# Order of the accumulating transfers in the GpSimd queue of an up-projection: sums of one pair interleaved with those of the next

## The chip, the cores and the metric

The kernel runs on one core of one Trainium2 chip. The metric is the time of one execution in microseconds of the device. The profile is that of one further execution, whose own time stands beside its span below.

## The reference

One layer of a diffusion backbone: a modulated input, three parallel token mixers, an output projection with residual and layer norm, and then the gated convolutional feed-forward network in which the change lies. There are 640 tokens (128 context, 512 latent), a model width of 1024 and a feed-forward width of 2816.

```python
def _conv_ffn(h, w_up, w_dw, b_dw, w_down, latent):
    a, g = jnp.split(h @ w_up, 2, axis=-1)
    ...
    conv = conv + b_dw
    return (jax.nn.gelu(conv) * g) @ w_down
...
    f = _conv_ffn(h2, p['w_up'], p['w_dw'], p['b_dw'], p['w_down'], latent)
    x = _layer_norm(alpha * x + g2 * f.astype(x.dtype), p['ln2_g'], p['ln2_b'])
```

`conv` is a 3x3 depthwise convolution on the latent grid and one of width 3 on the context.

## The kernel before

The last stage of the kernel, some 530 us of the profile, is the feed-forward network. Its width of 2816 is cut into 22 blocks j of 128 channels. For each block the up-projection makes two tiles, a (to be convolved) and g (the gate). Blocks 0 to 2 are made in the stage before, block 3 in plain form by `up_one`, and blocks 4 to 21 by `up_pair`, a *pair* each in what follows, being a and g of one block. A pair uses seven block products instead of eight (a Strassen form): tokens are cut into near (0 to 319) and far (320 to 639), the 1024 rows of the weights into a first and a second half, and sums of weight halves and of activation halves enter the products. Each product is 12 fp32r matmuls of TensorE (four tiles of 128 rows, three terms each: high times high, high times low, low times high), so a pair is 84 matmuls.

The weight sums are made by transfers that add to what they find (`onto`, line 1543, issued on GpSimd's queue, 128x512 elements each). Of a pair, `ra` and `rb` are buffers of the pool tag `sraw` (four buffers, so two pairs at a time), and `raw` is one of the streaming buffers; the first half of each is columns 0 to 511 (`f_`), the second columns 512 to 1023 (`s_`). SP loads `ra` (the weights of a, line 1559), `rb` (those of g, line 1560) and `raw` (those of g again, line 1569). The four sums are named here by number, and this text keeps to these names:

- sum1: first half of `rb` += first half of the weights of a, from memory (line 1561)
- sum2: second half of `rb` += first half of `rb` (line 1562); it needs sum1
- sum3: first half of `raw` += second half of the weights of g, from memory (line 1570)
- sum0: second half of `ra` += second half of `rb` (line 1595); it needs sum2, and it overwrites what the cast of a has read

Before TensorE can use a weight buffer, ScalarE casts it to a high part (`cast`, line 1587) and VectorE subtracts that for the low part (`low`, line 195). Per pair there are four such entries: a (`ra`), c (`rb`, after sum2), r (`raw`, after sum3) and t (the second half of `ra`, after sum0, 128x512). `advance` takes the next entry: it casts it, and leaves its low part and an *after* step to the next `settle`. The entries run one pair ahead: while `up_pair(j)` issues its seven products, a, c, r and t of pair j+1 are cast, in that order, at fixed places between the products.

The order on every engine is the order of the code here, as the stage is scheduled by hand. `up_pair` (from line 1705) goes: product with a onto xx, copy of xx by ScalarE (line 1717), second product with a, cast of the next a, then the products with c, r and t, each with copies or subtractions, and between them `pump`, which issues VectorE's taps of the convolution and, later, gelu (line 1665), gating (line 1669) and the split of the gated tile. The first product with c writes over xx and so has to wait for the copy at line 1717. At the end comes the copy at line 1743 and the cast of the next t.

Where transfers are issued in the kernel before: sum1 and sum2 of a pair right behind its loads (`load_pair`, called as *after* of t two pairs earlier), sum3 right behind its load (`load_raw`, called as *after* of r, or of a weight of the down-projection), and sum0 as *after* of a. An `rb` load needs the buffer that the low part of t has freed.

After pairs 7, 9 and 14 comes a down-projection over the blocks made so far (`down_part`): ten tiles of matmuls, whose scaled results (`ftmp`, two buffers) are added to `x1d` in memory by transfers on the same GpSimd queue. In it the entries of the next pair (a, c, then r, t) are cast at the last tile of each half.

Of the kernel before, what the change touches and what calls it, by code (L numbers as in the profile page):

```python
# [153 lines left out]
def layer_kernel(ctx, tc, wst, wada, par, cst, ftab, ttab, cond, x, state, sgub, wst_t, rows, bg, y, snew):  # L154
# [1386 lines left out]
    with tc.tile_pool(name="pu", bufs=1, reuse_waits="tile") as pu:  # L1541
# [11 lines left out]
        got_w, raws, pairs = {}, {}, {}  # L1553
        rest_raw, rest_pair, entries = [], [], []

        def load_pair(j):
            ia, ib = (plan.setdefault(("cm", "w_up", i * DFF + j * P), len(plan)) for i in range(2))
            ra, rb = pairs[j] = [pu.tile([P, 1024], F32, tag="sraw", bufs=SRAW, name=nm("sraw")) for _ in range(2)]
            nc.sync.dma_start(out=ra, in_=wst[ia])
            nc.sync.dma_start(out=rb, in_=wst[ib])  # L1560
            onto(rb[:, f_], wst[ia][:, f_])
            onto(rb[:, s_], rb[:, f_])

        def load_raw(key):
            kind, *a_ = key
            if kind == "r":
                ib = plan.setdefault(("cm", "w_up", DFF + a_[0] * P), len(plan))
                r = raws[key] = strm.tile([P, 1024], F32, tag="raw", name=nm("raw"))
                nc.sync.dma_start(out=r, in_=wst[ib])
                onto(r[:, f_], wst[ib][:, s_])  # L1570
            else:
                raws[key] = raw_weights("tm", "w_down", a_[0] * 512, 512, a_[1])
# [17 lines left out]
        def entry(key):  # L1590
            kind, *a_ = key
            if kind == "a":
                ra, rb = pairs[a_[0]]
                got_w[key], f = cast(ra)
                after = lambda: onto(ra[:, s_], rb[:, s_])
            elif kind == "c":
                got_w[key], f = cast(pairs[a_[0]][1])
                after = lambda: None
            elif kind == "t":
                got_w[key], f = cast(pairs.pop(a_[0])[0][:, s_], 512)  # L1600
                after = next_pair
            else:
                w, f = cast(raws.pop(key))
                got_w[key] = halves(w) if kind == "d" else w
                after = next_raw
            lows.append((f, after))
# [195 lines left out]
        with tc.manual_schedule(engines=MANUAL3 | {mybir.EngineType.Pool, mybir.EngineType.SP}):  # L1802
            next_pair()
            next_raw()
            next_pair()
            for j in (1, 0, 2):
                feed(j, [landed.pop((j, i)) for i in range(2)])
            advance()
            advance()
            settle()  # L1810
            next_raw()
            for kind, n in jobs:
                {"one": up_one, "pair": up_pair, "down": down_part}[kind](n)
# [114 lines left out]
```

## Time and profile before

| | us |
|---|---|
| median of 3 runs | 1302.96 |
| lowest and highest | 1300.44, 1307.67 |
| the profiled execution | 1306.42 |
| its span | 1304.6 |

| engine | busy us | share of the span |
|---|---|---|
| TensorE, matmuls | 1184.2 | 91% |
| VectorE | 887.8 | 68% |
| ScalarE | 509.9 | 39% |
| GpSimd | 91.7 | 7% |

Busy time of TensorE counts pipelined matmuls, so it is no measure of TensorE at its peak. Up to some 700 us TensorE is busy 96% to 100% of each 100 us; from 800 to 1200 us it is 74% to 83%, at a mean granted clock of 0.86 to 0.90 of full speed. That stretch holds pairs 4 to 19 and the three down-projections. In the rows below, PE is TensorE, DVE VectorE, ACT ScalarE, POOL GpSimd, and a trailing q stands for an engine's queue of instructions. A wait is attributed to the last event that the profile shows before it ends.

### The profile page before, as it was taken

To read this page: it belongs to the slowest core of one execution; us is meant where nothing else is said; L and a number is where in the kernel's file an instruction comes from. 1 tells how busy PE (TensorE), PEld (TensorE's weight loads), DVE (VectorE), ACT (ScalarE), POOL (GpSimd) and SP (SyncE) were. 2 spreads that over 40 slices of the span, in tenths; PEclk is the share of its full clock that TensorE was granted. 3 is DMA by queue.
4 is the path that set the end of the run, shared out by engine and by line. 5 is a ranking of instruction groups with operands and counts; after the bars stand their busy time and mean duration, and the time that the engine had idled before them with its cause. 6 is when DMAs were issued, how large, how long until landed. Compare 5 with 4: busy or idle time off the path is not lost. (4 is left out here: it accounts for less than half of the span.)

```text
span 1304.6 us, 19072 instructions
## 1 busy us (share of the span) xinstructions
PE 1184.2 (91%) x7535; PEld 1116.2 (86%) x7535; DVE 887.8 (68%) x1656; ACT 509.9 (39%) x844; POOL 91.7 (7%) x111
## 2 busy tenths in 40 slices
PE   9999999999999999999999996698696779867887
PEld 7999999999999999899988886687686768867876
DVE  7697576466775684988467866577664664456886
ACT  5576464334443222233235634343332431333520
POOL 0000000000000000000000002122122112211000
PEclk9999999999999999999999997799898889888989
DMA  9422212211252353534342226577675556765332
GB/s 350 167 69 68 80 49 73 73 57 50 83 197 86 109 167 129 175 112 166 97 161 98 98 99 128 137 176 132 159 135 125 135 148 119 163 146 117 123 121 84
DMA packets 54971, 161.80 MB, mean 124 GB/s; under 512 B 6233, under 2 KB 8665, under 8 KB 54881
## 3 DMA queue, kind: packets, MB, share of 16 engines
q1 hardware_dynamic: 39472, 131.22, 29.9%
q0 software_dynamic: 15408, 29.37, 13.5%
q8 instruction: 59, 0.97, 0.3%
q14 instruction: 32, 0.25, 0.1%
HBM read 136.97 MB, written 14.16 MB: 116 GB/s over the span
## 5 line engine op out<-in xcount | busy, mean ns | idle before, releaser
L195 DVE TENSOR_TENSOR wl<-raw,wh 128x1024 fp32r<-128x1024 f32 x123 | 148.0, 1204 | 84.9 <-ACT wh L219 75.9
L277 PE MATMUL up<-s,wh 128*128 128x320 f32 x216 | 76.8, 356 | 88.8 <-ACT fm L1717 88.8
L219 ACT CAST wh<-raw 128x1024 fp32r<-128x1024 f32 x83 | 85.0, 1027 | 168.3 <-PE gm L278 91.6
L277 PE MATMUL up<-go,wh 128*128 128x320 f32 (+2 forms) x384 | 124.2, 323 | 7.3 <-ACT fm L1755 6.3
L277 PEld LDWEIGHTS up<-s,wh 128*128 128x128 f32 x216 | 46.8, 217 | 93.3 <-ACT fm L1717 93.3
L278 PE MATMUL up<-go,wh 128*128 128x320 f32 (+2 forms) x384 | 123.1, 321 | 1.0 <-DVE go L195 1.0
L279 PE MATMUL up<-go,wl 128*128 128x320 f32 (+2 forms) x384 | 122.3, 318 | 0.4 <-DVE s11hv L307 0.4
L277 PE MATMUL gm<-h,wh 128*128 128x320 f32 x384 | 121.4, 316 | 0.0
L278 PE MATMUL gm<-h,wh 128*128 128x320 f32 x384 | 118.9, 310 | 0.0
L279 PE MATMUL gm<-h,wl 128*128 128x320 f32 x384 | 118.6, 309 | 0.0
L195 DVE TENSOR_TENSOR wl<-sraw,wh 128x1024 fp32r<-128x1024 f32 (+1 forms) x54 | 56.3, 1043 | 73.5 <-ACT wh L1587 73.1
L1657 DVE SCALAR_TENSOR_TENSOR cv<-fm,par,cv 128x441 f32<-128x441 f32 (+2 forms) x152 | 105.1, 691 | 1.7
L1587 ACT CAST wh<-sraw 128x1024 fp32r<-128x1024 f32 (+1 forms) x54 | 48.7, 903 | 127.4 <-DMA sraw<-sraw 101.5
L421 DVE SCALAR_TENSOR_TENSOR adac<-rawa,csil,adac 128x512 f32<-128x512 f32 x120 | 84.8, 744 | 10.3 <-DMA rawa<-in_wada 8.5
L277 PEld LDWEIGHTS up<-go,wh 128*128 128x128 f32 x384 | 76.8, 200 | 8.8 <-ACT fm L1755 6.6
L278 PEld LDWEIGHTS up<-go,wh 128*128 128x128 f32 x384 | 76.2, 199 | 2.4 <-DVE go L195 2.0
L279 PEld LDWEIGHTS up<-go,wl 128*128 128x128 f32 x384 | 75.8, 197 | 0.8 <-DVE s11hv L307 0.8
L277 PE MATMUL dn<-wh,h 128*128 128x512 f32 (+1 forms) x188 | 71.9, 383 | 2.5 <-ACT h L1671 1.6
L278 PE MATMUL up<-s,wh 128*128 128x320 f32 x216 | 74.2, 343 | 0.0
L279 PE MATMUL up<-s,wl 128*128 128x320 f32 x216 | 73.9, 342 | 0.0
L277 PEld LDWEIGHTS gm<-h,wh 128*128 128x128 f32 x384 | 72.1, 188 | 1.7 <-issue 1.2
L279 PE MATMUL dn<-wh,h 128*128 128x512 f32 (+1 forms) x188 | 71.6, 381 | 1.7 <-DVE h L195 1.6
(455 smaller groups left out, 3311.1 us busy)
## 6 DMA issues: line engine op xcount, KB each, us to landing
raw<-in_wst SPq DMA_DIRECT2D x134, 512.0 KB, 3.6
sraw<-in_wst SPq DMA_DIRECT2D x36, 512.0 KB, 4.5
rawa<-in_wada SPq DMA_DIRECT2D x32, 512.0 KB, 3.5
sraw<-sraw POOLq DMA_DIRECT2D x36, 256.0 KB, 4.2
wa<-in_wada SPq DMA_DIRECT2D x16, 512.0 KB, 8.0
x1d<-ftmp POOLq DMA_DIRECT2D x30, 256.0 KB, 4.1
sraw<-in_wst POOLq DMA_DIRECT2D x18, 256.0 KB, 4.1
raw<-in_wst POOLq DMA_DIRECT2D x18, 256.0 KB, 4.6
```

The lines of the kernel that those rows point to most:

```text
L195: V.tensor_tensor(out, src, hi.bitcast(F32), op=ALU.subtract)
L219: A.copy(wh[:, 0:n], r)
L277: PE.matmul(out, lhsT=l[0], rhs=r[0], start=start, stop=False, skip_group_check=onto)
L278: PE.matmul(out, lhsT=l[0], rhs=r[1], start=False, stop=False, skip_group_check=onto)
L279: PE.matmul(out, lhsT=l[1], rhs=r[0], start=False, stop=stop, skip_group_check=onto)
L421: MAC.scalar_tensor_tensor(acc_[:, cd], r[:, i], s_, acc_[:, cd], op0=ALU.mult, op1=ALU.add)
L1587: A.copy(wh[:, 0:n], r)
L1657: V.scalar_tensor_tensor(cg[:, r0:r1, c0:c1], ag[:, r0 + r - 1:r1 + r - 1, c0 + c - 1:c1 + c - 1], tap(r, c), cg[:, r0:r1, c0:c1], op0=ALU ...
```

## The change

The sums of the weights are no longer issued where their buffers are loaded. `load_pair` and `load_raw` put them into three lists, `sums1`, `sums2` and `sums3`, and the *after* steps take one from a list: that of a issues sum0 and then a sum1, that of r (and of a down weight) a sum2, that of t a sum3. `go` issues the next of a list, but no sum2 while the sum1 of its pair is not issued; `due` issues what an entry needs and is still in a list. At the start the first pairs' sums are issued by hand in the order shown.

```diff
--- before.py
+++ after.py
@@ -1552,14 +1552,25 @@
         jobs += [("pair", j) for j in range(10, 15)] + [("down", 2)] + [("pair", j) for j in range(15, NF)]
         got_w, raws, pairs = {}, {}, {}
         rest_raw, rest_pair, entries = [], [], []
+        sums1, sums2, sums3 = [], [], []
+
+        def go(*lists):
+            for l_ in lists:
+                if l_ and not (l_ is sums2 and sums1 and sums1[0][0] <= l_[0][0]):
+                    l_.pop(0)[1]()
+
+        def due(j, *lists):
+            for l_ in lists:
+                while l_ and l_[0][0] <= j:
+                    l_.pop(0)[1]()
 
         def load_pair(j):
             ia, ib = (plan.setdefault(("cm", "w_up", i * DFF + j * P), len(plan)) for i in range(2))
             ra, rb = pairs[j] = [pu.tile([P, 1024], F32, tag="sraw", bufs=SRAW, name=nm("sraw")) for _ in range(2)]
             nc.sync.dma_start(out=ra, in_=wst[ia])
             nc.sync.dma_start(out=rb, in_=wst[ib])
-            onto(rb[:, f_], wst[ia][:, f_])
-            onto(rb[:, s_], rb[:, f_])
+            sums1.append((j, lambda: onto(rb[:, f_], wst[ia][:, f_])))
+            sums2.append((j, lambda: onto(rb[:, s_], rb[:, f_])))
 
         def load_raw(key):
             kind, *a_ = key
@@ -1567,7 +1578,7 @@
                 ib = plan.setdefault(("cm", "w_up", DFF + a_[0] * P), len(plan))
                 r = raws[key] = strm.tile([P, 1024], F32, tag="raw", name=nm("raw"))
                 nc.sync.dma_start(out=r, in_=wst[ib])
-                onto(r[:, f_], wst[ib][:, s_])
+                sums3.append((a_[0], lambda: onto(r[:, f_], wst[ib][:, s_])))
             else:
                 raws[key] = raw_weights("tm", "w_down", a_[0] * 512, 512, a_[1])
 
@@ -1590,19 +1601,35 @@
         def entry(key):
             kind, *a_ = key
             if kind == "a":
+                due(a_[0], sums1, sums2)
                 ra, rb = pairs[a_[0]]
                 got_w[key], f = cast(ra)
-                after = lambda: onto(ra[:, s_], rb[:, s_])
+
+                def after():
+                    onto(ra[:, s_], rb[:, s_])
+                    go(sums1)
             elif kind == "c":
                 got_w[key], f = cast(pairs[a_[0]][1])
                 after = lambda: None
             elif kind == "t":
                 got_w[key], f = cast(pairs.pop(a_[0])[0][:, s_], 512)
-                after = next_pair
+
+
+                def after():
+                    next_pair()
+                    go(sums3)
             else:
+                if kind == "r":
+                    due(a_[0], sums3)
                 w, f = cast(raws.pop(key))
                 got_w[key] = halves(w) if kind == "d" else w
-                after = next_raw
+
+
+                def after():
+                    next_raw()
+                    go(sums2)
+                    if kind == "d":
+                        go(sums3)
             lows.append((f, after))
 
         def settle():
@@ -1802,13 +1829,16 @@
         with tc.manual_schedule(engines=MANUAL3 | {mybir.EngineType.Pool, mybir.EngineType.SP}):
             next_pair()
             next_raw()
+            go(sums1)
             next_pair()
+            go(sums2, sums3, sums1)
             for j in (1, 0, 2):
                 feed(j, [landed.pop((j, i)) for i in range(2)])
             advance()
             advance()
             settle()
             next_raw()
+            go(sums3)
             for kind, n in jobs:
                 {"one": up_one, "pair": up_pair, "down": down_part}[kind](n)
                 if kind == "one":
```

**GpSimd's queue in the last run of pairs.** Before the change, from sum0 of pair 18 on; `sraw_10784`, `sraw_10925`, `sraw_11066` and `sraw_11207` are rb of pairs 18 to 21, the `sraw` numbered one lower the ra of the same pair, and `raw` that of pairs 20 and 21:

```order
L1543 DMA sraw_10783<-sraw_10784 128x512
L1543 DMA raw_11038<-in_wst 128x512
L1543 DMA sraw_11066<-in_wst 128x512
L1543 DMA sraw_11066<-sraw_11066 128x512
L1543 DMA sraw_10924<-sraw_10925 128x512
L1543 DMA raw_11179<-in_wst 128x512
L1543 DMA sraw_11207<-in_wst 128x512
L1543 DMA sraw_11207<-sraw_11207 128x512
L1543 DMA sraw_11065<-sraw_11066 128x512
L1543 DMA sraw_11206<-sraw_11207 128x512
```

After the change, from the same sum on; the tiles of a pair carry numbers lower by one:

```order
L1543 DMA sraw_10782<-sraw_10783 128x512
L1543 DMA sraw_10924<-in_wst 128x512
L1543 DMA sraw_10924<-sraw_10924 128x512
L1543 DMA raw_11037<-in_wst 128x512
L1543 DMA sraw_10923<-sraw_10924 128x512
L1543 DMA sraw_11065<-in_wst 128x512
L1543 DMA sraw_11065<-sraw_11065 128x512
L1543 DMA raw_11178<-in_wst 128x512
L1543 DMA sraw_11064<-sraw_11065 128x512
L1543 DMA sraw_11206<-in_wst 128x512
L1543 DMA sraw_11206<-sraw_11206 128x512
L1543 DMA sraw_11205<-sraw_11206 128x512
```

Before, sum0 of pair 19 (`sraw_10924<-sraw_10925`) stands behind sum1 and sum2 of pair 20; now it stands ahead of both, behind sum3 of pair 20.

**GpSimd's queue at the start of the stage.** Before; `sraw_8266` and `sraw_8275` are rb of pairs 4 and 5, `raw_8271`, `raw_8289` and `raw_8355` belong to pairs 4, 5 and 6:

```order
L1543 DMA sraw_8266<-in_wst 128x512
L1543 DMA sraw_8266<-sraw_8266 128x512
L1543 DMA raw_8271<-in_wst 128x512
L1543 DMA sraw_8275<-in_wst 128x512
L1543 DMA sraw_8275<-sraw_8275 128x512
L1543 DMA sraw_8265<-sraw_8266 128x512
L1543 DMA raw_8289<-in_wst 128x512
L1543 DMA raw_8355<-in_wst 128x512
```

After, where rb of pair 5 is `sraw_8273`:

```order
L1543 DMA sraw_8266<-in_wst 128x512
L1543 DMA sraw_8266<-sraw_8266 128x512
L1543 DMA raw_8269<-in_wst 128x512
L1543 DMA sraw_8273<-in_wst 128x512
L1543 DMA sraw_8265<-sraw_8266 128x512
L1543 DMA raw_8288<-in_wst 128x512
L1543 DMA sraw_8273<-sraw_8273 128x512
L1543 DMA raw_8354<-in_wst 128x512
```

Sum0 of pair 4 (`sraw_8265<-sraw_8266`) stood behind sum2 of pair 5 and now stands ahead of it.

**GpSimd's queue in the first down-projection.** Before, from sum0 of pair 8 on; rb of pairs 8, 9 and 10 are `sraw_8709`, `sraw_8849` and `sraw_9205`, and `x1d` rows are the down-projection's own:

```order
L1543 DMA sraw_8708<-sraw_8709 128x512
L1543 DMA x1d_7123<-ftmp_9092 128x512
L1543 DMA x1d_7119<-ftmp_9111 128x512
L1543 DMA x1d_7120<-ftmp_9131 128x512
L1543 DMA x1d_7121<-ftmp_9149 128x512
L1543 DMA x1d_7122<-ftmp_9168 128x512
L1543 DMA x1d_7123<-ftmp_9198 128x512
L1543 DMA sraw_9205<-in_wst 128x512
L1543 DMA sraw_9205<-sraw_9205 128x512
L1543 DMA sraw_8848<-sraw_8849 128x512
```

After, from the same sum on:

```order
L1543 DMA sraw_8708<-sraw_8709 128x512
L1543 DMA sraw_8849<-in_wst 128x512
L1543 DMA x1d_7123<-ftmp_9091 128x512
L1543 DMA x1d_7119<-ftmp_9110 128x512
L1543 DMA x1d_7120<-ftmp_9130 128x512
L1543 DMA x1d_7121<-ftmp_9148 128x512
L1543 DMA x1d_7122<-ftmp_9167 128x512
L1543 DMA sraw_8849<-sraw_8849 128x512
L1543 DMA x1d_7123<-ftmp_9198 128x512
L1543 DMA sraw_8848<-sraw_8849 128x512
L1543 DMA sraw_9205<-in_wst 128x512
L1543 DMA sraw_9205<-sraw_9205 128x512
```

Sum1 and sum2 of pair 9 were issued during pair 7 and now stand between the down-projection's transfers; sum0 of pair 9 has moved ahead of sum1 and sum2 of pair 10.

TensorE, VectorE, ScalarE and SP have the same instructions in the same order before and after; only the numbers of the transfers that they wait for differ.

## Rows read from the trace of the kernel before

**Rows 1.** Table of waits, 780 us to the end: us in total, times, longest us.
```profile
POOL sraw L1543 <- DMA sraw<-in_wst: 146.8, 27, 11.7
ACT wh L1587 <- DMA sraw<-sraw: 101.5, 15, 12.8
...
PE up L277 <- ACT fm L1717: 88.8, 17, 10.8
...
POOL raw L1543 <- DMA raw<-in_wst: 48.7, 10, 7.5
POOL x1d L1543 <- DVE ftmp L1778: 48.1, 18, 6.3
```
**Rows 2.** Chain of waits, pair 18 to 19: start us, us, what.
```profile
1172.28 3.38 DMA sraw<-in_wst
...
1176.24 0.87 POOL sraw L1543
1177.11 4.24 issue
...
1181.90 7.02 DMA sraw<-sraw
...
1188.95 0.62 ACT wh L1587
```
**Rows 3.** Busy us (instructions) of PE, PEld, DVE, ACT, POOL; granted clock; DMA share; GB/s.
```profile
801.76:857.82 56.06, 43.17 (x252) 42.38 (x252) 39.17 (x60) 22.70 (x37) 8.71 (x10) 0.85 0.56 133
903.75:925.38 21.63, 14.12 (x84) 13.86 (x84) 15.55 (x24) 7.67 (x13) 3.48 (x4) 0.83 0.63 149
971.57:1055.06 83.49, 55.13 (x336) 54.08 (x336) 43.95 (x65) 28.89 (x47) 14.02 (x16) 0.85 0.60 142
1111.33:1209.46 98.13, 71.94 (x432) 70.62 (x430) 55.25 (x82) 36.76 (x57) 18.32 (x21) 0.86 0.62 144
1209.46:1223.67 14.21, 12.59 (x84) 12.33 (x84) 12.50 (x19) 7.78 (x13) 0.85 (x1) 1.00 0.22 54
1130.62:1191.73 61.11, 42.76 (x252) 41.97 (x252) 37.13 (x56) 23.31 (x38) 10.46 (x12) 0.84 0.58 134
867.00:900.00 33.00, 31.39 (x147) 26.02 (x145) 21.61 (x33) 7.23 (x9) 10.38 (x12) 1.00 0.76 135
925.38:937.98 12.60, 12.13 (x63) 12.04 (x64) 9.27 (x16) 6.53 (x11) 1.73 (x2) 0.75 0.65 184
1055.06:1067.67 12.61, 12.14 (x63) 12.05 (x64) 10.48 (x17) 5.87 (x10) 1.73 (x2) 0.75 0.55 155
857.82:867.81 9.99, 9.53 (x63) 9.45 (x64) 9.14 (x15) 6.22 (x11) 1.00 (x2) 1.00 0.75 215
```
**Rows 4.** ScalarE in order of time, pairs 20 and 21: start us, us, instruction, idle before.
```profile
1219.04 0.43 ACT L1743 COPY fm<-up 128x320 f32<-128x320 f32 x1 [0.85 <-PE up L279]
1219.36 0.62 ACT L1587 CAST wh<-sraw 128x512 fp32r<-128x512 f32 x1
1221.41 0.74 ACT L1665 ACTIVATE cv<-cv 128x640 f32<-128x640 f32 x1 [1.42 <-DVE cv L1657]
...
1223.67 0.42 ACT L1717 COPY fm<-up 128x320 f32<-128x320 f32 x1
...
1228.28 1.05 ACT L1587 CAST wh<-raw 128x1024 fp32r<-128x1024 f32 x1
```
**Rows 5.** VectorE in order of time, the same pairs.
```profile
1219.57 1.22 DVE L195 TENSOR_TENSOR wl<-raw,wh 128x1024 fp32r<-128x1024 f32 x1
...
1224.54 0.68 DVE L195 TENSOR_TENSOR wl<-sraw,wh 128x512 fp32r<-128x512 f32 x1
...
1226.78 1.22 DVE L195 TENSOR_TENSOR wl<-raw,wh 128x1024 fp32r<-128x1024 f32 x1
```
**Rows 6.** ScalarE in order of time, start of the stage.
```profile
788.53 1.04 ACT L1587 CAST wh<-sraw 128x1024 fp32r<-128x1024 f32 x1 [12.29 <-DMA sraw<-sraw]
...
799.80 0.62 ACT L1587 CAST wh<-sraw 128x512 fp32r<-128x512 f32 x1 [5.82 <-DMA sraw<-sraw]
```
## Prediction

> **What bounds the kernel now.** I read the table of waits of the last stage first, then the chain of waits, then the busy time by stretch, and last the order of single instructions on ScalarE and VectorE in the one pair that runs undisturbed.
>
> The waits say that TensorE stands still 88.8 us in all, at 17 of the 18 pairs, before the same matmul, for the copy at line 1717; that copy stands on ScalarE behind the cast of "t", and the casts wait 101.5 us for sums inside an `sraw` buffer. GpSimd itself waits 146.8 us for transfers into `sraw` [rows 1]. So an in-order queue of transfers sets the pace, and no engine does.
>
> The chain of waits shows the loop, here from the cast of t of pair 18 to that of pair 19: after the low part of t, the load of pair 20's rb is issued at 1172.28; its landing lets sum1 of pair 20 go at 1176.24; sum2 must await sum1, 4.24 us; and sum0 of **pair 19**, which needs nothing of pair 20, stands behind sum2 in the queue, lands 7.02 us later, and only then can t of pair 19 be cast, at 1188.95 [rows 2]. A pair's own last sum thus waits for a load and a sum of the next pair.
>
> What the loop costs is read from the stretches between the copies at line 1717, one per pair: 56.06 us for three periods, 21.63 for one, 83.49 for four and 98.13 for five, which is 259.31 us for 13 periods, 19.95 each. The fourteenth, from pair 20 to 21, where no further pair is loaded, takes 14.21 [rows 3]. In it TensorE is busy 12.59 us and VectorE 12.50, at a granted clock of 1.00 (2.4 GHz); in the others the clock is 0.83 to 0.86, that is, partly at 1.2 GHz after the stalls.
>
> **The change, part by part.** No transfer is added or removed. The rows on SP, TensorE, VectorE and ScalarE stay in their order; only GpSimd's queue is permuted, and SP's next ra load, which waits for sum0, can only start earlier. The price of an issue, 0.87 us of GpSimd [rows 2], stays, four to a pair; GpSimd was busy 10.46 us in 61.11 [rows 3], which covers it wherever it stands.
>
> *Sum0 of a pair now goes as soon as its a is split, ahead of sum1 of the next pair.* To see what is late next I lay the new order over the undisturbed pair. Count from the copy that ends pair 20, at 1219.04; in pair 21 weights of the last down-projection stand in the places of the next a, c and r. The cast of t begins 0.3 us later; the low part of r ends at 1.75; the low part of t at 6.2, which frees the buffer for the next rb load; the low part of a at 9.0; the cast of c begins at 9.2; the next cast of t is due at 14.5 [rows 4, 5]. So sum0, issued at 9.0, has 5.5 us. It has more in fact: the gelu behind t's cast waited another 1.42 us for VectorE [rows 4], so t may be late by that much free of cost, which makes 6.9. What it needs: sum1 alone took 0.87 + 4.24 us until sum2 could follow, and sum0 as the second of two took 7.02 from the end of the wait [rows 2]. With a load and at most the tail of one sum beside it, I take 5.5, nearer to the lone one. That fits.
>
> *Sum1 of the next pair now follows sum0.* Its load is issued at 6.2 and took 1176.24 - 1172.28 = 4.0 us [rows 2], so sum1 can go at about 10.3; it holds up nothing, as what stands behind it is its own sum2.
>
> *Sum2 is issued after the low part of the previous r*, at 1.75 or a little later; c needs it at 9.2, so it has 7.5 us where sums took 5.1 to 7.0. In the kernel before, it was ready most of a pair earlier. That is a wait which the change makes possible, and it costs nothing as long as a sum lands within 7.5.
>
> *Sum3 (for r) is issued after the low part of t*, at 6.2; its raw load is issued at 1.75 and must have landed, which it has by 5.8 if it takes the 4.0 us of the rb load. Before, GpSimd waited 48.7 us for raw loads, at most 7.5 at a time [rows 1]; a load of 6 us would leave it standing 1.6 here, and behind it is only sum0, due at 9.0.
>
> Nothing then keeps the pair from the 14.21 us of the undisturbed one, whose limit is VectorE's order (12.50 us busy plus two waits for ScalarE). I take 14.4, since its loads and sums now run closer together. **Pairs: 259.3 - 13 x 14.4 = 72.1 us gained.** The return of the clock is in this term, as the 14.21 were measured at 1.00.
>
> *The pairs that end a run.* Pair 9, entered after a long stall, took 12.60 us to its last copy at a clock of 0.75, and pair 14 took 12.61; pair 7, entered after a short one, took 9.99 at 1.00 [rows 3]. Pairs 9 and 14 should fall to that: **2 x 2.6 = 5.2 us gained.**
>
> *The first pair.* Its t waited 5.82 us for sum0 of pair 4, which stood behind sum2 of pair 5 and so behind sum1 of pair 5. Now it needs only its own sum2, whose landing let c be cast at 788.53; t was cast at 799.80 [rows 6]. At most the 5.8 us go; if VectorE's taps, already queued, become late instead, some 2 stay. I take **4 us gained.**
>
> *The first pair after a down-projection* inherits VectorE work: 15.55 us against 12.50 [rows 3]. That was hidden in the stall and is uncovered now; 0 to 3 us each, I take 1.6 for pairs 8, 10 and 15: **4.8 us given back.**
>
> *The down-projections.* A sum1 now stands among the accumulating transfers to x1d, and a sum2 ahead of the last of them. Both find their input landed long before, so they cost 0.87 us of issue each, and those transfers waited 48.1 us for VectorE there [rows 1], which covers it; without that cover it would be 1.7 us for each of three, 5 us.
>
> **Sum: 72.1 + 5.2 + 4 - 4.8 = 76.5 us**, and the profiled execution took 1306.4, so 1229.9, or 1230. That execution lies 3.5 us above the median of the runs shown, so a median may come out at 1226; the range takes it in.
>
> **Rivals.** *The transfers themselves become the bound.* Over three pairs the DMA engines were busy 0.58 of 61.11 us, 11.8 us a pair; the most they held over a long mixed stretch is 0.76, in the first down-projection [rows 3]. If that is their limit, a pair takes 11.8 / 0.76 = 15.5 us: 259.3 - 201.5 = 57.8, with 5.2 and 4 and nothing given back (the longer pair covers VectorE's backlog) 67, so 1239. For it: sums slowed one another, as the 7.02 shows. Against: a mean share of 0.83 is what my own forecast asks for, bursts have long gaps now, and pair 7 ran at 0.75 undisturbed. The Trainium skill, "DMA: Bandwidth & Descriptors", section "Issuing engines are not separate DMA queues", says that transfers issued by any engine run on the same 16 DMA engines and interleave; by that rule an order of issue changes who waits but not how much must be moved. The trace agrees in so far as a sum beside another took 7.02 us where one alone took 4.24.
>
> *The sums still stand in t's way*, because sum0 now waits behind sum3 for its raw load or behind sum2 of its own pair. Half of the loop's excess would stay, 17 us a pair: 259.3 - 221 = 38, with 3 for the start 41, so 1265. The 7.5 us longest wait for a raw load speak for it; that sum3 comes 2.8 us ahead of sum0 speaks against.
>
> *Slower: the wait moves from t to c.* If sum2, now issued late, lands so late that c holds up ScalarE, and with it the copies behind c, each pair waits there. The price is the lateness itself: a pair of 21 us needs a landing 6.8 us past the 7.5 it has, or 14.3, and gives 13 x 21 - 259.3 = 14 us more, so 1320. It turns slower than before at a landing of some 13.2 us. No sum in the chain took over 7.1, so little speaks for it.
>
> *It does nothing measurable*, if the sum was hidden behind a second wait of equal length, such as that for VectorE ahead of t: 1306. The undisturbed pair speaks against it.
>
> **How the numbers follow.** The forecast has 0.72, the DMA bound 0.18, the sums still in the way 0.06, slower 0.02, nothing 0.02. The forecast's own ends are 14.2 us a pair, the whole 5.8 at the start and nothing given back, 86 us, so 1221 and by the median's 3.5 some 1217; and the 5 us of uncovered issues with 3 us more behind each down-projection, 1240. With most of the DMA bound the range is 1215 to 1250; it leaves out the last three cases and the tails. About 0.5%, 6.5 us, is what a measurement of this kernel can tell from no change. Faster by more than that: 0.72 + 0.18 + 0.06 = 0.96; within it 0.02; slower by more 0.02.
>
> **What would show it right or wrong.** Right: TensorE's wait for the copy at line 1717 falls from 88.8 us to below 35; casts wait below 20 us for sums in `sraw`; the stretches of pairs show 14 to 15 us each, a clock near 1.00 and a DMA share above 0.75; in the chain of waits VectorE takes the place of the transfers. The DMA bound would show as casts of t or c waiting 1 to 2 us in each pair, with sums that take over 7 us. A new wait would show as casts from `sraw` at full width, c, waiting for a sum. I am wrong if the pairs stay above 16 us, or if the down-projections lengthen by more than 5 us each.

## The result, and the profile after

| | before | after |
|---|---|---|
| median, us | 1301.7 (4 runs) | 1232.28 (4 runs) |
| lowest and highest | 1299.67, 1307.67 | 1230.45, 1236.86 |
| the profiled execution, its span | 1306.42, 1304.6 | 1236.86, 1235.1 |
| mean granted clock | 0.958 | 0.981 |

The ratio is 0.9465, with a 95% interval of 0.9423 to 0.9506. The forecast was 1230, with a range of 1215 to 1250: it was right in sign and size. A second measurement of the same kernel beside the last experiments gave 1233.08 (0.9431, 0.9402 to 0.946).

By stage, from the starts of the near copy (line 1717 before, 1744 after) on ScalarE's timeline, in us. "Periods" are the 13 that were 56.06 + 21.63 + 83.49 + 98.13 in [rows 3]; "downs" run from the near copy of pairs 7, 9 and 14 to that of the next pair, and so hold the pair as well.

| | before | forecast | after | after, again |
|---|---|---|---|---|
| to the near copy of pair 4 | 801.8 | 797.8 | 798.2 | 797.9 |
| 13 periods | 259.3 | 192.0 | 191.0 | 188.4 |
| three downs | 148.4 | 143.2 | 149.8 | 150.2 |
| pair 20 | 14.2 | 14.2 | 14.2 | 14.2 |
| the rest | 80.9 | 80.9 | 81.8 | 79.8 |
| span | 1304.6 | 1228.1 | 1235.1 | 1230.5 |

Of the 69.5 us by which the span fell, 68.3 came from the pairs and 3.6 from the start; the downs and what follows gave some back. Windows of the changed kernel over the stretches of [rows 3] (the same columns); the first four are pairs 4 to 6, 8, 10 to 13 and 15 to 19, then comes pair 20, then the three downs:

```profile
798.23:839.62 41.39, 36.74 (x243) 35.71 (x244) 39.09 (x62) 23.04 (x37) 8.71 (x10) 1.00 0.73 178
888.90:903.38 14.48, 14.01 (x79) 14.02 (x80) 14.39 (x22) 7.67 (x14) 2.59 (x3) 0.80 0.81 188
947.97:1008.24 60.27, 53.19 (x344) 51.61 (x342) 43.78 (x65) 28.79 (x47) 14.64 (x17) 0.97 0.80 188
1064.21:1139.11 74.90, 66.43 (x432) 64.60 (x430) 56.77 (x85) 36.65 (x57) 18.83 (x23) 0.98 0.84 193
1139.11:1153.32 14.21, 12.59 (x84) 12.33 (x84) 12.51 (x19) 7.78 (x14) 1.24 (x2) 1.00 0.33 73
839.62:888.90 49.28, 41.64 (x215) 36.01 (x213) 34.49 (x54) 15.37 (x23) 13.02 (x15) 0.96 0.70 150
903.38:947.97 44.59, 41.50 (x205) 35.70 (x205) 34.02 (x51) 15.64 (x22) 12.24 (x15) 0.96 0.74 158
1008.24:1064.21 55.97, 53.87 (x254) 45.63 (x255) 32.59 (x46) 16.48 (x22) 11.19 (x14) 0.97 0.58 133
```

Five pairs now take 74.90 us, 14.98 each, where they took 98.13; the clock went from 0.86 to 0.98 and the DMA share from 0.62 to 0.84. Pair 20, which had no such wait, is the same 14.21 as before.

The waits of the changed kernel from 775 us on (us in total, times, longest) answer to [rows 1]:

```profile
POOL sraw L1543 <- DMA sraw<-in_wst: 89.4, 25, 7.1
...
ACT wh L1598 <- DMA sraw<-sraw: 30.2, 8, 12.2
...
PE up L277 <- ACT fm L1744: 22.8, 12, 6.7
```

TensorE's wait for the near copy fell from 88.8 to 22.8, the casts' wait for sums from 101.5 to 30.2, of which 12.2 is the very first c. GpSimd still stands 89.4 us for transfers into `sraw`. That costs nothing in the steady pairs (from 17 on no cast waits for a sum): what stands behind it is no longer the sum that is due next.

From the chain of waits over steady pairs of the changed kernel (start us, us, what):

```profile
1120.88 1.13 DVE wl L195
...
1122.63 0.75 ACT cv L1692
...
1123.41 0.84 DVE cv L1696
...
1124.27 0.73 ACT h L1698
```

No transfer is left in it from 1108 to 1126 us, where [rows 2] had 7.02 us for the landing of sum0. It is VectorE's work, with two trips to ScalarE (gelu, 0.75, and the cast of the gated tile, 0.73) for which VectorE has to wait.

### The profile page after: what moved, and what is told of

Its sections match the earlier page's. It is cut to its first block, busy times and chain, and to the rows that moved or that the text cites. A ratio compares the mean times of both kernels' runs of the same rounds, so it can differ in the third digit from the quotient of the medians.

```text
span 1235.1 us, 19074 instructions
## 1 busy us (share of the span) xinstructions
PE 1167.5 (95%) x7535; PEld 1098.2 (89%) x7535; DVE 886.1 (72%) x1656; ACT 510.3 (41%) x844; POOL 91.6 (7%) x111
## 4 chain that ended last, share of the span: by engine, by line
PE 60%; DVE 17%; DMA 10%; issue 6%; ACT 5%; POOL 1%; SPq 0%; DVEq 0%; ACTq 0%; POOLq 0%
DVE wl L195 5%; PE gm L277 5%; PE gm L278 5%; PE gm L279 5%; DVE cv L1684 4%; DMA raw<-in_wst 4%; DMA x1d<-ftmp 2%; PE pp L277 2%; PE pp L278 2%; PE pp L279 2%; PE dn L277 2%; PE dn L279 2%; PE dn L278 2%; PE up L277 2%; PE up L278 2%
## 5 line engine op out<-in xcount | busy, mean ns | idle before, releaser
L277 PE MATMUL up<-go,wh 128*128 128x320 f32 (+2 forms) x384 | 122.1, 318 | 13.9 <-ACT fm L1760 6.6
L278 PE MATMUL up<-go,wh 128*128 128x320 f32 (+2 forms) x384 | 120.5, 314 | 1.9 <-DVE go L195 1.9
L277 PE MATMUL up<-s,wh 128*128 128x320 f32 x216 | 69.6, 322 | 22.8 <-ACT fm L1744 22.8
L277 PEld LDWEIGHTS up<-go,wh 128*128 128x128 f32 x384 | 73.8, 192 | 17.5 <-ACT fm L1760 8.6
L277 PE MATMUL dn<-wh,h 128*128 128x512 f32 (+1 forms) x188 | 73.2, 389 | 4.0 <-ACT h L1698 2.8
L278 PEld LDWEIGHTS up<-go,wh 128*128 128x128 f32 x384 | 73.7, 192 | 3.4 <-DVE go L195 3.0
L279 PE MATMUL dn<-wh,h 128*128 128x512 f32 (+1 forms) x188 | 72.8, 388 | 1.9 <-DVE h L195 1.8
L277 PEld LDWEIGHTS gm<-h,wh 128*128 128x128 f32 x384 | 72.1, 188 | 1.7 <-issue 1.2
L1598 ACT CAST wh<-sraw 128x1024 fp32r<-128x1024 f32 (+1 forms) x54 | 48.8, 905 | 59.2 <-DMA sraw<-sraw 30.2
L278 PE MATMUL dn<-wl,h 128*128 128x512 f32 (+1 forms) x188 | 72.7, 387 | 0.0
L278 PEld LDWEIGHTS gm<-h,wh 128*128 128x128 f32 x384 | 72.2, 188 | 0.3
L279 PEld LDWEIGHTS gm<-h,wl 128*128 128x128 f32 x384 | 72.1, 188 | 0.0
```

Of the source, the lines that this page charges most:

```text
L277: PE.matmul(out, lhsT=l[0], rhs=r[0], start=start, stop=False, skip_group_check=onto)
L278: PE.matmul(out, lhsT=l[0], rhs=r[1], start=False, stop=False, skip_group_check=onto)
L279: PE.matmul(out, lhsT=l[1], rhs=r[0], start=False, stop=stop, skip_group_check=onto)
L1598: A.copy(wh[:, 0:n], r)
```

## The experiments

All ratios are to the kernel before on the same chip (medians there 1307.5, 1306.9 and 1306.6 for the three groups of runs). Sums of the stages by the same starts, from one profile each:

| kernel | median us | ratio, 95% interval | 13 periods | downs |
|---|---|---|---|---|
| sum0 behind sum1 | 1246.53 | 0.9526, 0.95 to 0.9551 | 205.6 | 147.4 |
| after, two taps fewer | 1223.09 | 0.9345, 0.932 to 0.9371 | 191.6 | 142.0 |
| before, two taps fewer | 1291.43 | 0.987, 0.9828 to 0.9912 | 255.8 | 139.0 |
| after, no sum3 | 1222.51 | 0.9344, 0.9323 to 0.9365 | 187.3 | 141.8 |
| after, half taps | 1215.96 | 0.9321, 0.928 to 0.9361 | 181.2 | 146.3 |
| before, half taps | 1305.62 | 0.9991, 0.9963 to 1.0019 | 256.6 | 148.5 |
| sum3 behind sum1 | 1237.11 | 0.9482, 0.9447 to 0.9517 | 194.3 | 150.7 |
| sum2 and sum3 behind sum1 | 1245.27 | 0.9544, 0.9507 to 0.9581 | 194.5 | 157.1 |
| late tail | 1230.21 | 0.9433, 0.9399 to 0.9468 | 179.5 | 157.8 |
| late tail, early ends | 1229.37 | 0.9397, 0.9365 to 0.9429 | 177.7 | 156.5 |
| the same, sum3 later | 1232.44 | 0.9433, 0.9403 to 0.9464 | 183.5 | 153.1 |
| after, again | 1233.08 | 0.9431, 0.9402 to 0.946 | 188.4 | 150.2 |

**Which queue order matters.** One part is undone: sum0 stands again behind sum1 of the next pair, which waits for its load, but still ahead of that pair's sum2.

```diff
                 def after():
-                    onto(ra[:, s_], rb[:, s_])
                     go(sums1)
+                    onto(ra[:, s_], rb[:, s_])
```

> The changed kernel with one exchange: sum1 of the next pair is issued just ahead of sum0 instead of just behind it. Theory (what held sum0 was all that stood ahead of it for the next pair: first the wait of sum1 for the rb load, then the wait of sum2 for sum1): the first of the two waits comes back. The load is landed some 10.3 us after the last copy of a pair, so sum0 goes at 11.2 and lands at 16 to 17.5 where t is due at 14.5 and may be late by 1.4. Pairs of 16 to 16.5 us instead of 14.7 on average; 1245 to 1262 us in all. Rival (only the wait of sum2 for sum1's landing mattered): sum1 ahead costs its issue of 0.87 us, pairs stay below 15 us, 1230 to 1238 us.

1246.53: at the near edge of what was expected. The 13 periods took 205.6 us against 259.3 and 191.0, so 53.7 of the 68.3 us are gained although sum0 still waits for an `rb` load. The wait for the load is worth the other 14.6 us. The 53.7 are 4.1 us a pair, close to the 4.24 us that sum2 stood for the landing of sum1 in [rows 2]; so that wait was most likely the costly one, though no run put sum2 alone back ahead of sum0. The 14.6 fall unevenly: pairs 17 to 19 take 14.21 to 14.93, while those behind a down take up to 19.1.

**Was VectorE a limit before, and is it one now?** First two of the eight grid taps were left out, in both kernels.

```diff
-            ops = [... if (r, c) != (1, 1)]
+            ops = [... if (r, c) not in ((1, 1), (0, 1), (2, 1))]
```

> The changed kernel without two of the ten taps of the convolution, (0,1) and (2,1), some 1.2 us of VectorE per block. Theory (VectorE's order now sets the pair): the steady pair falls from 14.21 to about 13.0 us; 1212 to 1225 us in all. Rival (DMA engines set it): the steady pair stays at 14.2 within 0.3 us and the whole within 4 us of the changed kernel's 1232.

> The kernel before without the same two taps. Theory (the loop through GpSimd's queue set the pair there): pairs stay at 19.5 to 20 us, the whole falls by 0 to 7 us, from the first pairs and the two last ones alone; 1295 to 1302 us. Rival (VectorE set a part of it): 1.2 us a pair, some 20 us in all, 1280 to 1285 us.

Inconclusive for the changed kernel: the time is inside the range of the theory, but it came from the downs (142.0 against 149.8), and the periods stayed at 191.6, though those after pair 14 fell from 14.98 to a mean of 13.8. Two steps fewer for `pump` also move gelu, gating and all that follows against the products. In pair 10 c waited 8.85 us for sum2. ScalarE's timeline there, and the transfers issued from 948 to 958 us (KB each, median us from issue to landing):

```profile
957.59 1.05 ACT L1598 CAST wh<-sraw 128x1024 fp32r<-128x1024 f32 x1 [8.85 <-DMA sraw<-sraw]
```

```profile
sraw<-in_wst SPq DMA_DIRECT2D x2, 512.0 KB
x1d<-ftmp POOLq DMA_DIRECT2D x2, 256.0 KB, 6.9
raw<-in_wst SPq DMA_DIRECT2D x1, 512.0 KB
sraw<-sraw POOLq DMA_DIRECT2D x1, 256.0 KB, 9.1
raw<-in_wst POOLq DMA_DIRECT2D x1, 256.0 KB, 6.4
```

Sum2 takes 9.1 us with three loads of 512 KB and three other accumulating transfers issued in the same 10 us; that is past the 7.5 us the prediction counted on for c. In the kernel before, the pairs stayed as the theory said (255.8 against 259.3), but the time fell more than expected, as the downs became 9.4 us shorter: they were left out of account.

So the same question again with the number of instructions kept: each grid tap computes half its columns only, in both kernels.

```diff
                 c0, c1 = max(0, 1 - c), GRID_W - max(0, c - 1)
+                c1 = c0 + GRID_W // 2
```

> The changed kernel with the eight grid taps of the convolution cut to half of their columns: as many instructions in the same order, each some 0.25 us shorter, 2 us of VectorE per block. Theory (VectorE sets the steady pair): the late pairs of a run fall from 14.21 to 12.4 to 12.8 us, where TensorE's 84 matmuls end; ratio to the kernel before 0.925 to 0.937, against 0.9465 of the changed kernel. Rival (transfers set it): the late pairs stay at 14.2, ratio 0.942 to 0.948.

> The kernel before with the grid's taps cut to half their columns (the output is no longer the convolution's): VectorE has some 2.5 us less work in each pair, in the same number of instructions. Theory (the pairs before were set by the order of the sums in GpSimd's queue): the thirteen periods stay at 250 to 259 us, 19.2 to 19.9 each, and only the down-projections and the last pair shorten; 1280 to 1300 us. Rival (VectorE was as much of a bound before as after): the periods fall by as much as in the changed kernel with half taps, 10 us or more in the sum.

This one tells the two apart. Before, 0.9991: VectorE's busy time over pairs 15 to 19 fell by 7 us (55.25 in [rows 3] to 47.98) and nothing came of it. After, 0.9321 against 0.9431 to 0.9465: some 16 us, of which 7 to 10 lie in the 13 periods (181.2 against 188.4 to 191.0), 4 in the downs and the rest at either end; the periods of the kernel before fell by 2.7. Windows over pairs 15 to 19, first of the kernel before with half taps, then of the changed kernel with half taps and, below it, of its pair 20:

```profile
1104.80:1207.30 102.50, 73.63 (x432) 72.32 (x430) 47.98 (x83) 36.74 (x58) 18.38 (x21) 0.85 0.61 138
```

```profile
1054.70:1124.10 69.40, 64.61 (x432) 63.03 (x430) 48.51 (x83) 36.55 (x57) 18.16 (x21) 1.00 0.86 204
1124.10:1136.80 12.70, 12.22 (x83) 12.22 (x84) 10.71 (x19) 7.69 (x14) 0.96 (x2) 1.00 0.37 85
```

The second fence shows what comes next as well. Pair 20 goes down to 12.70 us, of which TensorE is busy 12.22 at a clock of 1.00. (In the kernel before with half taps it took 14.02: behind a stall of 7.7 us TensorE was granted 0.88 there and was busy for 13.55.) Pairs 15 to 19 take 69.40 / 5 = 13.9 in the mean, and ScalarE waits for sums in that stretch:

```profile
ACT wh L1598 <- DMA sraw<-sraw: 6.8, 4, 2.8
```

So late sums are the next thing that lengthens a pair, though not all pairs: pair 18, with transfers beside it, took 12.69 like pair 20, while 16 and 19, in which c waited 2.3 and 2.8 us, took 15.24 and 15.50. The 13.9 is no fixed pace of the transfers either: the kernel "late tail, early ends" below moves as much and took 67.3 us for the same five pairs.

**Do the transfers fill the DMA engines?** Sum3 is left out altogether, a transfer of 256 KB less in each pair.

```diff
-                sums3.append((a_[0], lambda: onto(r[:, f_], wst[ib][:, s_])))
```

> The changed kernel without sum3, one of four sums of a pair, so that r is cast from the plain weights of g. Theory (transfers are not the bound): the steady pair stays at 14.2 us; only the second pair after a down-projection, where c and t waited 2 to 3 us each for sums, gets shorter; 1222 to 1231 us. Rival (transfers are the bound): 1.7 us less of 11.8 a pair, pairs of 12.5 to 13 us, 1208 to 1216 us.

The last pairs took 14.21, as with sum3, and all 13 periods 187.3 against 188.4 to 191.0: fewer bytes don't shorten a steady pair. The second pair after a down, which was expected to get shorter, did not: pair 11 took 18.08 (16.64 with sum3). Of the gain of some 10 us, 8 lie in the downs, 141.8 against 150: in the first of them 43.88 against 49.28. Its cause can be read on two engines of the changed kernel. GpSimd's timeline at the start of that down:

```profile
856.46 0.87 POOL L1543 DMA_DIRECT2D raw<-in_wst  x1 [14.75 <-DVE cv L1676]
860.12 0.86 POOL L1543 DMA_DIRECT2D raw<-in_wst  x1 [2.80 <-issue]
860.67 2.10 POOL L1543 DMA_DIRECT2D x1d<-ftmp  x2
```

and VectorE's, where the third `ftmp` needs the first transfer to have landed:

```profile
855.46 0.69 DVE L1805 SCALAR_TENSOR_TENSOR ftmp<-dn,g 128x512 f32<-128x512 f32 x1
...
867.20 0.69 DVE L1805 SCALAR_TENSOR_TENSOR ftmp<-dn,g 128x512 f32<-128x512 f32 x1 [8.51 <-DMA x1d<-ftmp]
```

Two sums into `raw` stand ahead of the first transfer to `x1d`, whose input was there from 856.1 (855.46 + 0.69) on; what released these sums the profile doesn't show (it names a tap for the first). Without them VectorE waits 3.06 us at that place:

```profile
858.87 0.69 DVE L1804 SCALAR_TENSOR_TENSOR ftmp<-dn,g 128x512 f32<-128x512 f32 x1 [3.06 <-DMA x1d<-ftmp]
```

**Other orders of the sums.** First sum3 behind sum1, as *after* of a, and no longer as *after* of a down weight; then sum2 there as well:

```diff
                     onto(ra[:, s_], rb[:, s_])
                     go(sums1)
+                    go(sums2)
+                    go(sums3)
...
                     next_raw()
-                    go(sums2)
-                    if kind == "d":
-                        go(sums3)
```

(the first without the line that adds `go(sums2)`, and with `go(sums2)` kept behind `next_raw()`).

> The changed kernel with sum3 of the first two pairs after a down-projection no longer issued right behind their loads (as after of a down weight) but behind sum0 and sum1 in the middle of the down-projection, and behind the low part of t. Theory (the first transfers of a down-projection into x1d stand in GpSimd's queue behind two sums that wait for raw loads, and VectorE waits for them for 8.5 us): the stretch from pair 7 to pair 8 falls from 49.3 to 42 to 45 us, that from 9 to 10 by 1 to 2, that from 14 to 15 by 0 to 3; ratio to the kernel before 0.937 to 0.943. Rival (the two ftmp buffers and VectorE's own backlog set it): stretches stay within 1 us of the changed kernel's, ratio 0.9465 within 0.003.

> The kernel of the run before this one, and sum2 issued right behind sum1 of the same pair, instead of behind the low part of r. Theory (sum2 being issued late is what lets c wait in the first two pairs after a down-projection, and elsewhere there is room either way): casts of c no longer wait after the down-projections, 2 to 3 us each at four places; steady pairs stay at 14.2; 4 to 8 us less than the run before, ratio 0.932 to 0.939. Rival (as in the kernel before, GpSimd standing at sum2 for sum1's landing holds up what is behind it): pairs lengthen by 1 us or more, ratio above 0.945.

Neither is better, and neither expectation held. With sum3 moved alone, the first down fell, by less than expected (46.41 against 49.28), but the second grew (47.96 against 44.59), and in pairs 11 and 16 c came late, so that these took 20.58 and 19.10 us. ScalarE's timeline in pair 11:

```profile
971.62 1.04 ACT L1598 CAST wh<-sraw 128x1024 fp32r<-128x1024 f32 x1 [6.88 <-DMA sraw<-sraw]
```

With sum2 behind sum1 as well, GpSimd stands at sum2 until sum1 has landed, as it did before the change: the steady pairs hold 14.2, but the first two downs lengthen to 50.61 and 51.71 (from 49.28 and 44.59). The waits of c, which were expected to go, grew to 5.9 and 5.4 us in pairs 11 and 16. GpSimd's timeline in the second of these downs, where sum2 and sum3 stand ahead of two transfers to `x1d`:

```profile
938.66 1.22 POOL L1543 DMA_DIRECT2D sraw<-in_wst  x1
943.67 0.86 POOL L1543 DMA_DIRECT2D sraw<-sraw  x1 [3.80 <-DMA sraw<-in_wst]
944.22 1.21 POOL L1543 DMA_DIRECT2D raw<-in_wst  x1
944.77 2.43 POOL L1543 DMA_DIRECT2D x1d<-ftmp  x2
```

**VectorE's waits for ScalarE.** `pump` in a pair issues gelu, gating and split only when enough taps lie between them, so that VectorE has other work while ScalarE answers:

```diff
-        def pump(n):
+        def pump(n, flush=True):
             while n and (taps_q or tail_q):
+                if not (taps_q or flush or age[0] >= tail_q[0][1]):
+                    return
...
-            pump(2)
+            pump(2, False)
```

(and so at each `pump` in `up_pair`). In the second kernel the last argument is true in pairs 7, 9 and 14. In the third, sum3 is also issued ahead of the next load in a down, one weight later than in the changed kernel:

```diff
-            pump(2, False)
+            pump(2, j in ENDS)
...
+                    if kind == "d":
+                        go(sums3)
                     next_raw()
                     go(sums2)
-                    if kind == "d":
-                        go(sums3)
```

> The changed kernel, where gelu, gating and the split of a gated tile are not issued ahead of time when no tap is left in the list, but wait for the taps of the next block, so that VectorE has a tap to do while ScalarE does the gelu and the cast. Theory (the steady pair is VectorE's 12.5 us plus two round trips to ScalarE of 0.8 us each): late pairs fall from 14.21 to 12.6 to 13.4 us, eight of them; ratio 0.937 to 0.943. Rival (at such a pace sums and loads become late): casts wait for sums in every pair, late pairs 13.8 to 14.2, ratio 0.944 to 0.948.

> As the late-tail kernel, but in the pair ahead of each down-projection the gelu, gating and split are issued as early as in the changed kernel, so that they aren't left for the down-projection. Theory (VectorE's two waits for ScalarE set the pair of 14.2, and the late tail lost its gain in the third down-projection, where TensorE waited 6.6 us for h): the thirteen periods stay near 180 us, the third down-projection falls from 64.7 back to 56 to 58, and the time is 1219 to 1226. Rival (a faster pair only reaches the down-projection's weights sooner, and their loads land when they did): the third down-projection stays above 61 us, 1228 to 1234.

> As the kernel with the late tail and early ends, but in a down-projection sum3 is issued one weight later, ahead of the next load and not right behind its own, so that GpSimd doesn't stand at it with the down-projection's transfers to x1d behind it. Theory (VectorE's waits of 8.5 us for those transfers come from GpSimd standing at sum3 for its load): the first and third down-projection fall by 3 to 5 us each, 1213 to 1220. Rival (the transfers would land late anyway, or r is now late): no gain, within 3 us of the kernel with early ends, with casts from raw waiting for a sum.

The periods do fall, from 191.0 to 179.5 and 177.7, several to between 12.1 and 13.1, as the theory of VectorE's waits for ScalarE has it. The time follows only in part: 0.9433 lies between the two ranges expected for the first of these kernels. The third down takes 64.7 and 63.0 us instead of 56.0, and the early ends don't help: TensorE waits there for the gated tile of block 13 (this down works on blocks 8 to 13) as long as without them. Its timeline in the second kernel:

```profile
1023.42 0.80 PE L277 MATMUL dn<-wh,h 128*128 128x512 f32 x1 [6.55 <-ACT h L1698]
```

In the changed kernel that wait is 1.51 us and ends at 1022.70. The near copy of pair 14 came 5.8 us earlier here (1002.40 against 1008.24), and the tile that the down needs came no earlier: TensorE had run ahead of VectorE, and the down collects the debt. So the expectation for the early ends failed, and the rival's numbers came true, though not by its mechanism: the wait is for the tile, not for a load. That VectorE's backlog is too old by pair 14 to be caught up in one pair is argued, not shown. With sum3 later, the first down fell by 3.6 us (48.77 to 45.17; VectorE's wait at that place from 7.66 to 4.43), but the third did not (63.50 against 63.00), and pair 11 gave 6 back (12.67 to 18.92); as a whole this expectation failed too.

Beside these, the changed kernel once more:

> The changed kernel once more, unaltered, beside the two that build on it. Expected 1230 to 1237 us and a ratio of 0.942 to 0.951, thirteen periods of 191 us in all, down-projections (with the pair ahead) of 49, 45 and 56 us. If the periods differ by more than 2 us each from the first profile, the differences of a few us between kernels in single profiles mean nothing.

Its stages differ from the first profile's by up to 2.6 us, and single downs by up to 1.5; smaller differences between single profiles mean nothing here. 1229.37 with early ends and 1233.08 for the changed kernel have overlapping intervals: no version tried is shown to be faster than the change.

## Why the prediction was right

*Pairs: 259.3 - 13 x 14.4 = 72.1 us.* The mechanism was the one named: sum0 stood in GpSimd's queue behind sum2 of the next pair, and that behind the landing of sum1. With sum0 ahead of them the wait is gone, and the undisturbed pair was the right measure of the steady ones: pairs 13, 18 and 19 took 14.20 to 14.21 in both profiles. Together with the 4.8 us of backlog the forecast was 192.0; 191.0 and 188.4 were measured. That the sum came so close is in part luck, as single pairs run from 12.56 (pair 5) to 16.64. The backlog was put in the wrong pair: pairs 8, 10 and 15 took 14.48, 14.30 and 14.92, hardly more than the 14.4; the excess came one pair later (16.64 in pair 11, 16.44 in pair 16), and there ScalarE's timeline shows c waiting for sum2, in pair 15 also t for sum0:

```profile
969.95 1.04 ACT L1598 CAST wh<-sraw 128x1024 fp32r<-128x1024 f32 x1 [2.97 <-DMA sraw<-sraw]
...
1078.60 0.62 ACT L1598 CAST wh<-sraw 128x512 fp32r<-128x512 f32 x1 [3.17 <-DMA sraw<-sraw]
...
1086.61 1.04 ACT L1598 CAST wh<-sraw 128x1024 fp32r<-128x1024 f32 x1 [2.77 <-DMA sraw<-sraw]
```

So the rival "the wait moves from t to c" is real, but small: after the very first, c waits 1.6 to 3.0 us, in pairs 6, 10, 11, 15 and 16 alone. So is the rival of the sums that still stand in t's way: t waits 2.7 and 3.2 us, at the end of pairs 10 and 15. All but pair 6 are the two pairs next behind the second and third down.

*The clock in pairs 9 and 14: 5.2 us.* This term failed in the total, not in the pair: the second and third down together fell by 1.9 us in one profile and by 2.1 in the other. Pair 14 ran at 1.00 from its near copy to its last one and took 9.99 us for it (1008.24 to 1018.23) where it had taken 12.61; pair 9 took 10.7 for 12.60. What the step left out is what stood ready behind: the casts of the down's weights now wait for their loads. ScalarE's timeline of the changed kernel at the end of pairs 9 and 14:

```profile
912.68 1.05 ACT L1598 CAST wh<-raw 128x1024 fp32r<-128x1024 f32 x1 [1.91 <-DMA raw<-in_wst]
...
1016.30 1.05 ACT L1598 CAST wh<-raw 128x1024 fp32r<-128x1024 f32 x1 [1.59 <-DMA raw<-in_wst]
```

And the rest of the second and third down, from that last copy on, was granted 0.95 and 0.96 in that profile, where it had 1.00 in the kernel before. Windows over that rest of the third down, before and, in the second fence, after:

```profile
1067.67:1111.33 43.66, 42.77 (x192) 35.05 (x192) 24.15 (x33) 10.64 (x13) 10.38 (x12) 1.00 0.64 123
```

```profile
1018.23:1064.21 45.98, 44.35 (x193) 36.19 (x192) 22.83 (x31) 10.61 (x13) 11.19 (x14) 0.96 0.56 113
```

The 2.3 us lost there eat most of the 2.6 won in pair 14. In the second profile of the same kernel the third down took 54.47 us, 1.8 less than before; the second, 45.88, is 0.3 less than before.

*The first pair: 4 us.* 3.5 and 3.9 by the two profiles.

*The down-projections at no cost.* This term was wrong for the first, which became 3.4 to 4.0 us longer (49.28 and 49.89 for 45.93). Sum3 in front of `x1d` is not new as a wait: VectorE waited 8.84 us at that place in the kernel before as well. Its timeline of the kernel before, at the third and the seventh `ftmp`:

```profile
883.86 0.69 DVE L1778 SCALAR_TENSOR_TENSOR ftmp<-dn,g 128x512 f32<-128x512 f32 x1 [8.84 <-DMA x1d<-ftmp]
...
894.58 0.69 DVE L1778 SCALAR_TENSOR_TENSOR ftmp<-dn,g 128x512 f32<-128x512 f32 x1 [0.57 <-DMA x1d<-ftmp]
```

After the change the third stands at 867.20 (above); the seventh, and ahead of it two transfers of GpSimd's queue:

```profile
879.70 0.69 DVE L1805 SCALAR_TENSOR_TENSOR ftmp<-dn,g 128x512 f32<-128x512 f32 x1 [2.35 <-DMA x1d<-ftmp]
```

```profile
873.23 1.21 POOL L1543 DMA_DIRECT2D sraw<-in_wst  x1
873.78 1.54 POOL L1543 DMA_DIRECT2D x1d<-ftmp  x1
```

Counted from the near copy of pair 7, the third `ftmp` comes at 27.6 us where it came at 26.0, and the seventh at 40.1 where it came at 36.8 (27.9 and 40.7 in the second profile). So 1.5 of the 3.4 us arise ahead of the third: VectorE reaches the first one 1.9 us later (at 15.8 in place of 14.0), as it enters pair 7 with work of pair 6 still to do, which in the kernel before it did in the stall for t. The step counted such backlog only behind the downs. The other 1.8 arise at the seventh, which waits for the transfer of the fifth; that transfer now stands right behind sum1 of pair 9. The step priced sum1 there at its issue, covered by GpSimd's waits; what grew is the time until the transfer behind it had landed. The kernel with sum0 behind sum1 shows the two parts apart: there t stalls again ahead of pair 7, the first `ftmp` comes at 14.0 as before, the seventh still waits 2.1 us, and the down takes 47.67 us. No run moved this sum1 alone, so its part is read from the order.

*The signs.* The wait for the copy came out at 22.8 (below 35 forecast), VectorE in the chain in place of the transfers as forecast, the pairs at 12.6 to 16.6, wider than the 14 to 15 forecast, with a mean of 14.7. The casts' wait of 30.2 missed the 20. The DMA bound of 15.5 a pair fell: it rested on 0.76 as the most the DMA engines could hold, and five pairs held 0.84, those with half taps 0.86. Its sign, casts that wait for sums, did show behind the second and third down, where the share was highest: 0.99 in pair 10, 1.05 in pair 15. A share above 1 also says that this figure doesn't end at 1, so no limit can be read off it. The window of pair 15:

```profile
1064.21:1079.13 14.92, 14.28 (x96) 13.78 (x94) 7.21 (x10) 5.68 (x10) 4.48 (x6) 1.00 1.05 243
```

The rule of the Trainium skill, "DMA: Bandwidth & Descriptors", section "Issuing engines are not separate DMA queues", that transfers of all issuers share the same 16 DMA engines, is tested by no run here. The trace is in keeping with it: by share and length, five pairs come to 0.62 x 98.13 = 60.8 us of DMA time before and 0.84 x 74.90 = 62.9 after. The order changed who waited, not what was moved.

## What to carry to other kernels

A queue that issues in order, as GpSimd's does here, makes every entry wait for the landing of whatever the entry ahead waits for: write down for each transfer when its input is there and when its result is due, and let nothing that still waits for its input stand ahead of something that is due sooner. What such a fix is worth is read from a stretch in which the wait is absent (here one pair of 14.21 us among pairs of 20), since that stretch shows where the next limit lies; a cut in the suspected next limit, made in the kernel before and in the one after, then tests it (no measurable change before; some 16 us after, 7 to 10 of them in the pairs). Ahead of a stage boundary, a faster loop gets earlier to what the next stage waits for and leaves it more of the slower engine's work, so the boundary needs its own account.

## What the runs showed of the hardware

A sum of 256 KB took longer to land in the changed kernel, where the same transfers are packed more densely (DMA share over pairs 15 to 19 of 0.84 against 0.62) and in another order; no run separates the two. The table of DMA issues of the kernel before and, in the second fence, of the changed kernel (KB each, median us from issue to landing):

```profile
sraw<-sraw POOLq DMA_DIRECT2D x36, 256.0 KB, 4.2
...
sraw<-in_wst POOLq DMA_DIRECT2D x18, 256.0 KB, 4.1
```

```profile
sraw<-sraw POOLq DMA_DIRECT2D x36, 256.0 KB, 4.7
...
sraw<-in_wst POOLq DMA_DIRECT2D x18, 256.0 KB, 5.0
```

In one place, with three loads and three more such transfers issued within the same 10 us, it was 9.1 us (above), twice the median.

The granted clock fell in one profile of the changed kernel and not in the other, after the same thing on TensorE. At the start of the third down TensorE was busy 3.49 of 5 us, then came this; windows of the first profile, then of the second:

```profile
1018.00:1023.00 5.00, 3.49 (x15) 2.58 (x15) 3.29 (x5) 3.00 (x5) 0.00 (x0) 1.00 0.39 147
1023.00:1028.00 5.00, 4.88 (x14) 3.49 (x13) 4.12 (x7) 0.48 (x1) 0.86 (x1) 0.66 0.45 116
```

```profile
1017.50:1022.50 5.00, 3.42 (x16) 2.50 (x15) 3.21 (x5) 2.92 (x5) 0.00 (x0) 1.00 0.45 150
1022.50:1027.50 5.00, 4.87 (x21) 3.67 (x21) 4.20 (x7) 0.55 (x1) 0.86 (x1) 1.00 0.43 114
```

A stretch at the lower of the two levels (1.2 against 2.4 GHz) brings 0.66 in the mean of the first, with 14 matmuls where the other has 21. The down took 55.97 us in the first and 54.47 in the second, 1.5 us apart; 0.34 of 5 us is 1.7. By this estimate a hole of 1.5 us in TensorE's work cost about as much again through the clock, and in another execution nothing. The same was seen behind the wait of c in pair 11, which was alike in both profiles (2.97 and 2.81 us): pair 12 in the first profile, then in the second:

```profile
978.91:994.03 15.12, 14.13 (x84) 13.86 (x84) 12.60 (x19) 7.76 (x13) 3.45 (x4) 0.89 0.81 179
```

```profile
979.34:993.54 14.20, 12.58 (x84) 12.32 (x84) 12.50 (x19) 7.77 (x14) 3.45 (x4) 1.00 0.79 184
```
